# Loading all of x but its first 128 columns over ScalarE's DMA queue in a one-core encoder layer

## The chip, the core and the metric

The kernel runs on one core of one Trainium2 chip. The metric is the device time of one execution in microseconds (us), lower is better. Times come from runs without a profile. The rows come from one profiled execution of the kernel before.

## What is computed

One layer of a streaming encoder, on x of 512 rows by 1024 columns, all in float32. The part around the change is the first norm and the first projection:

```
hn   = rmsnorm(x, norm_mix_g)            # x * rsqrt(mean(x*x)) * g
proj = hn @ w_in                         # (512 x 1024) @ (1024 x 3592)
fq, fk, fv, ff, gq, gf, gi, gg = split(proj)
h = x + concat(fox_attention(fq, fk, fv, ff), hgrn2(gq, gf, gi) * silu(gg)) @ w_out
h = h + memory_cross_attention(rmsnorm(h), rmsnorm(mem))
h = h + square(relu(rmsnorm(h) @ w1)) @ w2
out = rmsnorm(h)
```

## The kernel before

Matrix products are made of two-part numbers. A weight panel of 1024 rows by 256 columns is loaded as two halves of 512 rows ("a" and "b", tiles `wr..`). ScalarE copies each into a rounded part (`wh..`, line 166), VectorE makes the remainder (`wl..`, line 168), and three matmuls (lines 227 to 229) stand for one product. The stretch of the change is the first 25 us.

x lies in one tile `xt`. For each of its eight blocks of 128 columns, `x_T(c)` (line 399) makes four TensorE transposes into a PSUM tile `xn`, `x_hi(c)` on ScalarE (line 402) and `x_lo(c)` on VectorE (line 405) turn that into the two parts `hn_hi` and `hn_lo`. The orders of TensorE, ScalarE and VectorE are written out by hand here: `x_T(0)`, `x_T(1)`, then the cast of the first weight quarter, then the parts of blocks 0 and 1. After that a loop over c makes the six matmuls of block c into the two accumulators `gf`, and then the transposes and parts of block c + 2, with other jobs behind them (`jobs`). Six matmuls `warm` stand ahead of all that on TensorE, and need no loaded data.

Loads are issued by an engine's own queue, in program order, SyncE's (SP) for nearly all. The first panel is loaded in four quarters of 256 KB (`load_next(4, ...)`), and the hook `more_x` puts a piece of x behind each of the first three. So SP's queue holds x[0:128] (256 KB), the first quarter of the weights, x[128:256] (256 KB), x[256:512] (512 KB), the second quarter, x[512:768] (512 KB), the third quarter, x[768:1024] (512 KB), the last quarter: 3 MB. Behind them come five small loads (`rows`) and the halves of the next panel (`wr1a`, `wr1b`). ScalarE's queue holds one small load (`gmr`), issued ahead of the engine's table load. Loads over SP and ScalarE take their completion semaphores in turn from a set of eight, DMAHW0 to DMAHW7; a load that gets one for the second time waits on its issuing engine until the load that had it before has landed.

Of the kernel before, what the change touches and what calls it, by code (L numbers as in the profile page):

```python
# [16 lines left out]
P = 128  # L17
# [5 lines left out]
WT = 256  # L23
# [19 lines left out]
def emit(  # L43
# [21 lines left out]
    nc = tc.nc  # L65
    te, ve, ac, gp = nc.tensor, nc.vector, nc.scalar, nc.gpsimd

    x, mem, w_in, w_out = x[0], mem[0], w_in[0], w_out[0]
# [36 lines left out]
    def t2(name, dt=F32, shape=(S,)):  # L105
        return t2p.tile([P] + list(shape), dt, tag="t2", name=name)
# [65 lines left out]
    def load_unit(name, spec, ks, parts=1, between=None):  # L172

        nw = max(sl.stop for sl, _ in spec)
        hi, lo = new_parts([UK, nw], name)
        raw_ = wrp.tile([P, UK * nw], F32, tag="wr", name=f"wr{name}", padded_shape=[P, UK * UW])
        raw_ = raw_.rearrange("p (k n) -> p k n", k=UK)
        nk = UK // parts
        splits = []
        for q in range(parts):  # L180
            qs, src_ks = slice(q * nk, (q + 1) * nk), slice(ks.start + q * nk, ks.start + (q + 1) * nk)
            for sl, src in spec:
                nc.sync.dma_start(raw_[:, qs, sl], src[:, src_ks, :])
            if between is not None:
                between(q)
            splits.append(split_of(hi[:, qs, :], lo[:, qs, :], raw_[:, qs, :]))
        return (hi, lo), splits

    def load_next(parts=2, between=None):

        i = len(stream)
        if i >= len(specs):
            return []
        units, splits = [], []
        for n in range(2):
            note = None if between is None else (lambda q, n=n: between(n * parts // 2 + q))
            unit, some = load_unit(f"{i}{'ab'[n]}", specs[i], slice(n * UK, (n + 1) * UK), parts // 2, note)
            units.append(unit)
            splits += some
        stream.append(tuple([u[x] for u in units] for x in range(2)))  # L200
        return splits
# [98 lines left out]
    xt = ap_.tile([P, NT, D], F32, tag="act", name="xt")  # L300
    gmr = t2("gmr", F32, (P,))[0:KC, :]
    ac.dma_start(gmr, norm_mix_g[0].rearrange("(k p) -> k p", p=P))

    def load_x(g, n=WT):
        gs = slice(g, g + n)
        nc.sync.dma_start(xt[:, :, gs], x[:, gs].rearrange("(t p) n -> p t n", p=P))

    def more_x(q):
        if q == 0:
            load_x(P, P)  # L310
        if q < 3:
            load_x((q + 1) * WT)

    load_x(0, P)
    first = load_next(4, more_x)
    rows = t2("rows", F32, (P,))[0:33, :]
    for r, src in ((0, norm_x_g), (8, norm_mem_g), (16, norm_ff_g)):
        nc.sync.dma_start(rows[r : r + 8, :], src[0].rearrange("(k p) -> k p", p=P))
# [590 lines left out]
    for n in range(len(units) + LAG):  # L909
        if n < len(units):  # L910
            p, tb, j = units[n]
# [492 lines left out]
```

## Time and profile before

| what | value |
|---|---|
| median of 3 runs | 786.74 us (785.2 to 787.53) |
| profiled execution, its own time | 784.74 us |
| span of its trace, first to last instruction | 783.0 us |
| TensorE busy | 770.4 us |
| HBM read | 88.14 MB |

The span leaves out some 1.7 us around the first and last instruction. A share of busy time is an average over all stages, so the first stage is to be read from its own rows. In a row of the timeline the first number is the start from the span's beginning, the second is a length, both in us; "xt<-in_x_dram" is the tile written and what is read; in square brackets stands how long the engine was idle before it and what it waited for. On a DMA queue's row (SPq, ACTq) the length is that of the issue, not of the transfer.

### The profile page before, as it was taken

To read this page: it belongs to the slowest core of one execution; us is meant where nothing else is said; L and a number is where in the kernel's file an instruction comes from. 1 tells how busy PE (TensorE), PEld (TensorE's weight loads), DVE (VectorE), ACT (ScalarE), POOL (GpSimd) and SP (SyncE) were. 2 spreads that over 40 slices of the span, in tenths; PEclk is the share of its full clock that TensorE was granted. 3 is DMA by queue.
4 is the path that set the end of the run, shared out by engine and by line. 5 is a ranking of instruction groups with operands and counts; after the bars stand their busy time and mean duration, and the time that the engine had idled before them with its cause. 6 is when DMAs were issued, how large, how long until landed. Compare 5 with 4: busy or idle time off the path is not lost.

```text
span 783.0 us, 11532 instructions
## 1 busy us (share of the span) xinstructions
PE 770.4 (98%) x4380; PEld 655.1 (84%) x4380; DVE 519.9 (66%) x839; ACT 367.6 (47%) x626; POOL 184.8 (24%) x259
## 2 busy tenths in 40 slices
PE   8999999999999999999999999999999999999996
PEld 5889998978989988888888888888888888888875
DVE  4746755687577656645538646959596877778662
ACT  5655455675565443244434344435353534344433
POOL 7106332414433005410006420100101010100013
PEclk9999999999999999999999999999999999999999
DMA  7543322242443443312222596575748475753302
GB/s 238 193 123 107 98 56 55 82 115 75 162 135 122 148 136 108 107 55 81 70 65 81 179 264 150 155 177 157 183 150 200 136 197 136 194 146 111 77 1 108
DMA packets 80777, 100.43 MB, mean 128 GB/s; under 512 B 4513, under 2 KB 62410, under 8 KB 80722
## 3 DMA queue, kind: packets, MB, share of 16 engines
q1 hardware_dynamic: 72002, 76.08, 30.7%
q0 software_dynamic: 8128, 22.57, 13.5%
q10 hardware_dynamic: 592, 1.05, 0.4%
q8 instruction: 34, 0.56, 0.3%
q14 instruction: 21, 0.17, 0.1%
HBM read 88.14 MB, written 4.21 MB: 118 GB/s over the span
## 4 chain that ended last, share of the span: by engine, by line
PE 96%; DVE 1%; DMA 1%; ACT 1%; issue 0%; POOL 0%; SPq 0%; POOLq 0%
PE u L229 7%; PE u L227 7%; PE u L228 7%; PE U L1280 3%; PE U L1279 3%; PE U L1278 3%; PE xq L227 2%; PE xw L227 2%; PE xw L229 2%; PE xq L229 2%; PE xq L228 2%; PE xw L228 2%; PE wo L227 2%; PE wo L228 2%; PE wo L229 2%; PE Y L1280 2%
## 5 line engine op out<-in xcount | busy, mean ns | idle before, releaser
L168 DVE TENSOR_TENSOR wld<-wq,whd 128x1024 fp32r<-128x1024 f32 x49 | 59.7, 1219 | 24.5 <-ACT whd L166 24.4
L227 PE MATMUL u<-x_hi,whu 128*128 128x512 f32 x192 | 74.7, 389 | 0.0
L228 PE MATMUL u<-x_lo,whu 128*128 128x512 f32 x192 | 74.7, 389 | 0.0
L229 PE MATMUL u<-x_hi,wlu 128*128 128x512 f32 x192 | 74.7, 389 | 0.0
L166 ACT ACTIVATE whd<-wq 128x1024 fp32r<-128x1024 f32 x49 | 51.0, 1051 | 23.7 <-PE u L228 22.1
L166 ACT ACTIVATE whu<-wru 128x1024 fp32r<-128x1024 f32 x24 | 25.3, 1052 | 56.8 <-DMA wru<-in_w_dram 56.8
L168 DVE TENSOR_TENSOR wlu<-wru,whu 128x1024 fp32r<-128x1024 f32 x24 | 29.3, 1220 | 26.4 <-ACT whu L166 26.2
L1156 POOL DMA_DIRECT2D wq<-wq x14 | 12.3, 878 | 136.7 <-DVE wld L168 96.9
L1156 POOL DMA_DIRECT2D wq<-in_w_dram x14 | 17.0, 1217 | 114.4 <-DMA wq<-in_w_dram 99.2
L1278 PE MATMUL U<-whd,hb 128*128 128x512 f32 x112 | 43.6, 389 | 0.0
L1279 PE MATMUL U<-wld,hb 128*128 128x512 f32 x112 | 43.6, 389 | 0.0
L1280 PE MATMUL U<-whd,hb 128*128 128x512 f32 x112 | 43.6, 389 | 0.0
L228 PEld LDWEIGHTS u<-x_lo,whu 128*128 128x128 f32 x192 | 36.0, 188 | 7.5
L227 PEld LDWEIGHTS u<-x_hi,whu 128*128 128x128 f32 x192 | 36.0, 188 | 7.5
L229 PEld LDWEIGHTS u<-x_hi,wlu 128*128 128x128 f32 x192 | 36.0, 188 | 7.4
L1216 ACT ACTIVATE sq<-ur 128x512 f32<-128x512 f32 x32 | 20.0, 626 | 29.1 <-DVE ur L1213 29.1
L1213 DVE SCALAR_TENSOR_TENSOR ur<-u,rbc 128x512 f32<-128x512 f32 x32 | 21.9, 688 | 17.2 <-PE u L229 17.2
L850 POOL TENSOR_SCALAR bi<-nF,Ft 128x128 f32<-128x128 f32 (+3 forms) x32 | 21.3, 664 | 43.0 <-PE pt L877 25.2
L867 ACT ACTIVATE bi<-bi,mx 128x128 f32<-128x128 f32 (+3 forms) x32 | 17.9, 560 | 20.9 <-DVE mx L865 20.6
L1279 PEld LDWEIGHTS U<-wld,hb 128*128 128x128 f32 x112 | 21.0, 188 | 4.4
L1278 PEld LDWEIGHTS U<-whd,hb 128*128 128x128 f32 x112 | 21.0, 188 | 4.4
L1280 PEld LDWEIGHTS U<-whd,hb 128*128 128x128 f32 x112 | 21.0, 188 | 4.3
(950 smaller groups left out, 2452.6 us busy)
## 6 DMA issues: line engine op xcount, KB each, us to landing
wq<-in_w_dram SPq DMA_DIRECT2D x39, 512.0 KB, 3.3
wru<-in_w_dram SPq DMA_DIRECT2D x24, 512.0 KB, 3.8
wq<-in_w_dram POOLq DMA_DIRECT2D x14, 512.0 KB, 8.7
wq<-wq POOLq DMA_DIRECT2D x14, 512.0 KB, 4.6
xTd<-xT POOLq DMA_DIRECT2D x4, 512.0 KB, 3.0
nF<-Fd POOLq DMA_DIRECT2D x8, 256.0 KB, 3.8
hT<-xTd POOLq DMA_DIRECT2D x4, 512.0 KB, 3.5
xt<-in_x_dram SPq DMA_DIRECT2D x3, 512.0 KB
```

What stands on the lines that cost most here:

```text
L166: ac.activation(hi, raw, AF.Copy)
L168: ve.tensor_tensor(lo, raw, f(hi), ALU.subtract)
L227: te.matmul(ps, wh, hi, start=n_ == 0, stop=False)
L228: te.matmul(ps, wh, lo, start=False, stop=False)
L229: te.matmul(ps, wl, hi, start=False, stop=n_ == KC - 1)
L850: gp.tensor_scalar(bi[:, 0:n], fF[h][:, 0:n], -1.0, Ft[:, tb, h : h + 1], op0=ALU.mult, op1=ALU.add)
L1156: gp.dma_start(raw.rearrange("p (k n) -> p k n", k=2), src, accum_op=ALU.add)
L1213: ve.scalar_tensor_tensor(u, ps, 0.0, rbc2, op0=ALU.max, op1=ALU.mult)
L1216: ac.activation(sqs[g, j][:, i, :], u, AF.Square)
L1278: te.matmul(ps, hi, whi[:, k, :], start=first_ and k == 0, stop=False, skip_group_check=True)
L1279: te.matmul(ps, hi, wlo[:, k, :], start=False, stop=False, skip_group_check=True)
L1280: te.matmul(ps, lo, whi[:, k, :], start=False, stop=k == 1, skip_group_check=True)
```

## The change

All pieces of x but the first are now issued over ScalarE's queue, ahead of the weights in the program. The hook `more_x` goes, so that the four weight quarters follow x[0:128] directly on SP.

```diff
-    def load_x(g, n=WT):
+    def load_x(g, n=WT, queue=ac):
         gs = slice(g, g + n)
-        nc.sync.dma_start(xt[:, :, gs], x[:, gs].rearrange("(t p) n -> p t n", p=P))
-
-    def more_x(q):
-        if q == 0:
-            load_x(P, P)
-        if q < 3:
-            load_x((q + 1) * WT)
-
-    load_x(0, P)
-    first = load_next(4, more_x)
+        queue.dma_start(xt[:, :, gs], x[:, gs].rearrange("(t p) n -> p t n", p=P))
+
+    load_x(0, P, nc.sync)
+    load_x(P, P)
+    for q in range(1, 4):
+        load_x(q * WT)
+    first = load_next(4)
```

ScalarE, from the start of the program, before (L166 is the cast of a weight quarter, L402 `x_hi`):

```order
L302 DMA gmr_113<-in_norm_mix_g_dram 8x128
L166 ACT_TABLE_LOAD
L166 ACTIVATE wh0a_116<-wr0a_118 128x512 [waits DMAHW2_49]
L402 ACTIVATE hn_hi_187<-xn0_205,g_mix_201 128x512 [waits DVE_49,PE_49]
L402 ACTIVATE hn_hi_187<-xn1_210,g_mix_201 128x512 [waits PE_49]
L402 ACTIVATE hn_hi_187<-xn2_229,g_mix_201 128x512 [waits PE_49]
L166 ACTIVATE wh0a_116<-wr0a_118 128x512 [waits DMAHW5_49]
```

The same place in the changed kernel, whose lines below the edit have numbers that are 3 lower (L399 is `x_hi`):

```order
L302 DMA gmr_113<-in_norm_mix_g_dram 8x128
L306 DMA xt_112<-in_x_dram 128x4x128
L306 DMA xt_112<-in_x_dram 128x4x256 x2
L306 DMA xt_112<-in_x_dram 128x4x256 [waits DMAHW2_49]
L166 ACT_TABLE_LOAD
L166 ACTIVATE wh0a_120<-wr0a_122 128x512 [waits DMAHW3_49]
L399 ACTIVATE hn_hi_187<-xn0_205,g_mix_201 128x512 [waits DVE_49,PE_49]
L399 ACTIVATE hn_hi_187<-xn1_210,g_mix_201 128x512 [waits PE_49]
L399 ACTIVATE hn_hi_187<-xn2_229,g_mix_201 128x512 [waits PE_49]
L166 ACTIVATE wh0a_120<-wr0a_122 128x512 [waits DMAHW5_49]
```

Four issues now stand ahead of the table load, and the fourth of them (x[768:1024]) has a wait. DMAHW2 is the semaphore of x[128:256] there.

SP's queue from the start, before (L183 loads weights, L306 x):

```order
L306 DMA xt_112<-in_x_dram 128x4x128
L183 DMA wr0a_118<-in_w_in_dram 128x2x256
L306 DMA xt_112<-in_x_dram 128x4x128
L306 DMA xt_112<-in_x_dram 128x4x256
L183 DMA wr0a_118<-in_w_in_dram 128x2x256
L306 DMA xt_112<-in_x_dram 128x4x256
L183 DMA wr0b_126<-in_w_in_dram 128x2x256
L306 DMA xt_112<-in_x_dram 128x4x256 [waits DMAHW0_49]
L183 DMA wr0b_126<-in_w_in_dram 128x2x256 [waits DMAHW1_49]
...
L319 DMA rows_130<-in_hgrn_norm_g_dram 1x128 [waits DMAHW5_49]
L320 DMA rows_130<-in_hgrn_lb_logits_dram 8x128 [waits DMAHW6_49]
L183 DMA wr1a_274<-in_w_in_dram 128x4x256 [waits DMAHW7_49,DVE_49]
```

And in the changed kernel:

```order
L306 DMA xt_112<-in_x_dram 128x4x128
L183 DMA wr0a_122<-in_w_in_dram 128x2x256 x2
L183 DMA wr0b_127<-in_w_in_dram 128x2x256
L183 DMA wr0b_127<-in_w_in_dram 128x2x256 [waits DMAHW0_49]
L315 DMA rows_130<-in_norm_x_g_dram 8x128 [waits DMAHW1_49]
...
L316 DMA rows_130<-in_hgrn_norm_g_dram 1x128 [waits DMAHW5_49]
L317 DMA rows_130<-in_hgrn_lb_logits_dram 8x128 [waits DMAHW6_49]
L183 DMA wr1a_274<-in_w_in_dram 128x4x256 [waits DMAHW7_49,DVE_49]
```

The four pieces of x are gone from between the weights. In the kernel before, DMAHW5 belonged to the second weight quarter and DMAHW6 to x[512:768], DMAHW7 to the third quarter; now DMAHW7 belongs to x[512:768].

One more thing moves by itself, on GpSimd (POOL), where the scheduler sets the order. Before, the small load `fb` (128 copies of 8 numbers) is issued near the start:

```order
masks.py:199 AFFINE_SELECT ident<-ident 128x128 [waits Pool_49]
L380 AFFINE_SELECT tri<-tri 128x128 [waits Pool_49]
L377 TENSOR_TENSOR id_182<-ident 128x64 [waits Pool_49]
L385 DMA fb<-in_fox_f_bias_dram 128x8
L367 MEMSET mkf_150 128x384
```

In the changed kernel the masks (`mkf`) come first, and `fb` stands after them:

```order
L369 AFFINE_SELECT mkf_166<-mkf_166 128x64
L374 TENSOR_TENSOR id_182<-ident 128x64
L377 AFFINE_SELECT tri<-tri 128x128
L370 AFFINE_SELECT mkf_166<-mkf_166 128x64 [waits Pool_49]
L382 DMA fb<-in_fox_f_bias_dram 128x8
```

So `fb` leaves the first microseconds. The orders of TensorE and VectorE are the same in both kernels, apart from the numbers of the semaphores.

## Rows read from the trace of the kernel before

**Rows 1.** Page, parts 1 and 4: busy shares, and the chain that ended last.

```profile
PE 770.4 (98%) x4380; PEld 655.1 (84%) x4380; DVE 519.9 (66%) x839; ACT 367.6 (47%) x626; POOL 184.8 (24%) x259
...
PE 96%; DVE 1%; DMA 1%; ACT 1%; issue 0%; POOL 0%; SPq 0%; POOLq 0%
```

**Rows 2.** The chain that ended last, first 30 us: start, length, what.

```profile
2.32 7.60 DMA xt<-in_x_dram
...
9.96 0.67 PE xn L399 x4
```

**Rows 3.** Timeline of SP's queue from the start: start, length of the issue, line, transfer.

```profile
0.79 0.42 SPq L306 DMA_DIRECT2D xt<-in_x_dram  x1
1.27 0.50 SPq L183 DMA_DIRECT2D wr0a<-in_w_in_dram  x1
1.81 1.01 SPq L306 DMA_DIRECT2D xt<-in_x_dram  x2
...
3.93 0.90 SPq L183 DMA_DIRECT2D wr0b<-in_w_in_dram  x1
...
5.82 2.03 SPq L183 DMA_DIRECT2D wr0b<-in_w_in_dram  x1
...
10.69 0.22 SPq L319 DMA_DIRECT2D rows<-in_hgrn_norm_g_dram  x1
12.21 0.27 SPq L320 DMA_DIRECT2D rows<-in_hgrn_lb_logits_dram  x1
13.02 0.40 SPq L183 DMA_DIRECT2D wr1a<-in_w_in_dram  x1
```

**Rows 4.** Timeline of ScalarE and its queue from the start.

```profile
0.79 0.61 ACTq L302 DMA_DIRECT2D gmr<-in_norm_mix_g_dram  x1
1.44 1.28 ACT L166 ACT_TABLE_LOAD   x1 [1.44 <-PEq L1390]
5.20 0.63 ACT L166 ACTIVATE wh0a<-wr0a 128x512 fp32r<-128x512 f32 x1 [2.48 <-DMA wr0a<-in_w_in_dram]
...
17.13 1.05 ACT L422 ACTIVATE x0j<-xt 128x1024 f32<-128x1024 f32 x1
```

**Rows 5.** Timeline of TensorE from the start.

```profile
1.30 2.74 PE L327 MATMUL warm<-zero 128*128 128x512 bf16 x6 [1.30 <-DVE zero L324]
...
4.32 1.11 PE L399 MATMUL xn<-ident,xt 128*128 128x128 f32 x4
6.03 0.66 PE L399 MATMUL xn<-ident,xt 128*128 128x128 f32 x4 [0.59 <-DMA xt<-in_x_dram]
6.46 0.49 PE L227 MATMUL gf<-hn_hi,wh0a 128*128 128x512 f32 x1
...
8.07 0.40 PE L228 MATMUL gf<-hn_lo,wh0a 128*128 128x512 f32 x1
8.30 0.39 PE L229 MATMUL gf<-hn_hi,wl0a 128*128 128x512 f32 x1
9.96 0.66 PE L399 MATMUL xn<-ident,xt 128*128 128x128 f32 x4 [1.27 <-DMA xt<-in_x_dram]
...
14.07 0.60 PE L399 MATMUL xn<-ident,xt 128*128 128x128 f32 x4
```

**Rows 6.** DMA issues: transfer, queue, count, KB each, median us from issue to landing.

```profile
out_dram<-fo SPq DMA_DIRECT2D x4, 256.0 KB, 2.6
xt<-in_x_dram SPq DMA_DIRECT2D x2, 256.0 KB, 2.8
wr0b<-in_w_in_dram SPq DMA_DIRECT2D x2, 256.0 KB, 9.1
```

**Rows 7.** Timeline, end of the span: both output queues, and TensorE's last matmul.

```profile
775.67 0.28 PE L1296 MATMUL y<-whd7b,hb 128*128 128x256 f32 x1
...
778.83 0.37 ACTq L1322 DMA_DIRECT2D out_dram<-fo  x1
778.86 0.33 SPq L1324 DMA_DIRECT2D out_dram<-fo  x1
```

**Rows 8.** Windows: stretch, length, busy of five engines, granted TensorE clock, DMA share, GB/s.

```profile
776.00:780.00 4.00, 0.00 (x0) 0.00 (x0) 1.16 (x2) 1.23 (x3) 0.85 (x2) 1.00 0.08 30
780.00:781.00 1.00, 0.00 (x0) 0.00 (x0) 0.00 (x0) 0.00 (x0) 0.00 (x0) 0.67 1.01 387
```

**Rows 9.** Timeline of ScalarE at a later table load, and the activation behind it.

```profile
155.34 1.28 ACT L867 ACT_TABLE_LOAD   x1
156.63 0.40 ACT L867 ACTIVATE bi<-bi,mx 128x128 f32<-128x128 f32 x1
```

## The prediction

> **What bounds the kernel now.** I read the busy shares first: TensorE is busy for 770.4 of 783.0 us, and 96% of the chain that ended last is its own [rows 1]. So a load matters only where TensorE stands still for it, and a standstill at the start moves all that follows by its length. The chain of the first 30 us shows one: 7.60 us of DMA into xt, up to 9.96 [rows 2]. Then the timeline of TensorE: it waits 0.59 us for x[128:256] (until 6.03) and 1.27 us for x[256:512] (until 9.96); from 14.07 on it goes from block to block with no wait shown [rows 5]. Last, the timelines of the two queues, for what stands in front of what [rows 3, 4].
>
> The landings in the order of SP's queue, read from whoever stopped waiting, with the sum of KB issued up to there: first weight quarter, 512 KB, 5.20 [rows 4]; x[128:256], 768 KB, 6.03 and x[256:512], 1280 KB, 9.96 [rows 5]; second quarter, 1536 KB, 10.69; x[512:768], 2048 KB, 12.21; third quarter, 2304 KB, 13.02, the wait of wr1a [rows 3]; last quarter, 3072 KB, 14.9, from its issue at 5.82 plus 9.1 [rows 3, 6]. I use this list as a scale: a transfer that ends when so many KB in all have been moved lands at about that time. It is an estimate, since it was made with one queue.
>
> **What must be in time.** The transposes of block 2 stand behind the six matmuls of block 0, and the first of these began 1.26 us after the first weight cast did (6.46 against 5.20), the last at 8.30 [rows 4, 5]. One step takes 0.23 us (8.07 to 8.30), so TensorE was free for block 2 at 8.53, or 3.33 us after that cast's start. The cast had until 9.96 - 3.33 = 6.63 to begin, and began at 5.20 [rows 4, 5]: 1.43 us to spare.
>
> **What the change adds on ScalarE.** Four issues stand ahead of its table load, and the fourth waits for x[128:256] to land, because its semaphore is given out a second time. Behind that wait stand the table load, the first cast, and the parts of blocks 0 and 1, for which VectorE and TensorE wait. The three issues without a wait end by about 2.9 us: 1.40 (0.79 + 0.61, [rows 4]) plus three at 0.5 (1.01 for two, [rows 3]); that is hidden, as nothing there is needed before 5.20. The wait is not hidden. With L for the landing of x[128:256], the cast begins at L + 0.05 + 0.47 (one issue; 0.42 to 0.50 where the queue is not full, 0.90 where it is, [rows 3]) + 0.04 + 1.28 (table load, [rows 4]) = L + 1.84.
>
> L is not in the trace. At the least it is 4.2: issue at 1.40 plus 2.8 for 256 KB with nothing in front [rows 4, 6]. At the most it comes after x[0:128] and all weights, at 1536 KB on the scale: 10.69. Between them I look at the only place where both queues carry like loads: the last two outputs, 256 KB each, are issued 0.03 us apart on ScalarE's and SP's queues [rows 7], the SP ones land 2.6 us after issue, against 2.8 for one alone [rows 6], and 387 GB/s flow meanwhile [rows 8]. So neither queue stands behind the other, and I take half of the flow for each. x[128:256] starts 0.6 us later than x[0:128], so by its end SP has moved 256 KB and a lead of some 150, 660 in all. If the queues take turns row by row, x's 512-byte rows against the weights' 1 KB rows, SP gets more, and it is some 830. The middle, about 750, is where this load stood before (768), so I leave L at 6.03.
>
> The rule of the Trainium skill, DMA: Bandwidth & Descriptors, section "Issuing engines are not separate DMA queues", speaks against the change: loads from several engines run on the same 16 DMA engines and interleave, and only the time to issue them is saved. The pair of outputs agrees. By that rule the forecast stands; were it wrong, the early landing below would be the likelier case.
>
> **The sum.** The cast begins at 6.03 + 1.84 = 7.87, TensorE is free for block 2 at 7.87 + 3.33 = 11.20, 1.24 us later than 9.96. x[256:512] itself: by half shares 512 KB of it come with 512 KB of weights, so it ends at 750 + 1024 = 1774 KB, on the scale 10.69 + 238/512 x (12.21 - 10.69) = 11.40 [rows 3]. The later of the two decides: 11.40, which is **1.44 us later**. Before, this load had only 1280 KB up to its end: it was near the front of one queue, and now shares with weights that are not needed yet.
>
> What is gained is worth nothing. The second quarter lands sooner, but its cast stands on ScalarE behind `x_hi(2)`, which follows block 2's transposes; the third and last quarters were waited for by no engine that mattered. What comes later is covered: x[512:768] ends at 1280 + 1280 = 2560 KB, some 13.7 on the scale, and is needed at 14.07 + 1.44 = 15.5 [rows 5]; wr1a's issue, which now waits for it, still waits for VectorE's work as well and moves no more than the rest; x[768:1024] ends last, at 14.9, and the sum of squares that reads it came at 17.13 [rows 4], now 18.6. If that cover were gone, each would cost its own lateness. The move of fb is off every wait in the first 60 us; I cost it at nothing, but it may quicken the loads.
>
> After block 2 every engine is shifted alike, so 1.44 us reach the end: 784.74 + 1.44 = 786.18 for an execution like the profiled one. That one lies 2.00 below the median of 786.74, within what single runs differ by; on the median it is **788.2 us**.
>
> **Rivals.**
>
> *The clock falls (slower).* TensorE would stand still from 6.69 (end of block 1's transposes, 6.03 + 0.66, [rows 5]) to 7.87 + 1.26 = 9.13: 2.44 us, where the longest standstill before was 1.27 and left it at full speed. For it: after the last matmul, over at 775.95 [rows 7], the granted clock holds 1.00 (2.4 GHz) over 776 to 780 and is 0.67 on the mean in the next microsecond [rows 8], so a standstill of about 4 us does bring 1.2 GHz. Against it: 2.44 lies nearer to 1.27 than to 4. Price: at the start the engine is slow from 1.30 until at least 5.43, by the same four transposes taking 1.11 us at 4.32 and 0.66 at 6.03 [rows 5]; 4.1 us at half speed lose 2.1 us of work. 786.74 + 1.44 + 2.1 = 790.3. It decides once that standstill counts as idle, and grows if x[128:256] is late.
>
> The Trainium skill, TensorE: Matmul & The Clock Gate, Part 1, says that the throttled state is the default and activity releases it; the trace's end agrees, and no row shows it for 2.44 us.
>
> *Early landing (no change).* If ScalarE's queue gets all it can take, x[128:256] lands at 4.2, the cast begins at 6.04 and TensorE is free at 9.37; x[256:512] then ends at 1024 KB, on the scale 8.0 [rows 5]. Gain 0.59: 786.2. The sequence on ScalarE allows no more, so a gain over 0.3% (2.36 us, about what a measurement of this kernel can tell from no change) is not in this change.
>
> *The weights go first (slower).* With L at 10.69 block 2 starts at 10.69 + 1.84 + 3.33 = 15.86: 5.90 later, 792.6. SP issues first and its queue holds 1280 KB, but the pair of outputs speaks against it.
>
> *A longer table load (slower).* In the trace the activation behind a table load starts 0.01 us after it ends [rows 9], so a wait behind the load would be a new one; if one as long as the load (1.28) came, the cast would begin at 9.15 and block 2 at 12.48: 2.52 later, 789.3. The Trainium skill, ScalarE: Activation LUTs, section "What ACT_TABLE_LOAD costs", adds a drain of about 1.38 us to each load, and by it block 2 would come at 12.58; the row at 155.34 shows none.
>
> **How the numbers follow.** Forecast 0.50 (of it 0.43 within 0.3%, 0.07 slower, since 788.2 is 0.9 below the bound of 789.1 and runs scatter by 1); clock 0.22 (0.20 slower, 0.02 within); early landing 0.17 (0.14 within, 0.03 faster by scatter); weights first 0.07, all slower; table load 0.04 (0.03 slower, 0.01 within). In sum: faster 0.03, same 0.60, slower 0.37. The range leaves out the weights-first case (0.07), the upper end of the clock case (0.05) and the lower half of the early landing (0.07): 785.9 to 790.6.
>
> **What would show it.** Right: ScalarE's table load stands behind the issue of x[768:1024] at about 6.1 to 6.6, the first cast starts near 7.9, block 2's transposes near 11.4, and from there every row is some 1.4 us later. Block 2's transposes waiting for DMA says that sharing decides; starting right after the matmuls says that the table load does. Wrong: a cast before 6.6 (no loss), gf matmuls 0.43 us apart instead of 0.23 (the clock), x[128:256] after 7 (the weights).

## The result, and the profile after

| | before | after |
|---|---|---|
| median, us (10 runs each) | 785.28 (783.8 to 787.53) | 787.45 (786.47 to 788.69) |
| ratio, 95% interval | | 1.0032 (1.0023 to 1.0041) |
| profiled execution, us | 784.74 | 786.47 |
| its span, us | 783.0 | 784.8 |

The change makes the kernel slower by 2.5 us (1.8 to 3.2, from the ratio). The prediction was 1.44 us more, at 788.2, and it gave "within 0.3%" 0.60 and "slower" 0.37. The measured time lies in its range. The ratio is just past the bound of 0.3%, with an interval that reaches to both sides of it, so between those two cases it decides nothing. But the loss is larger than the sum of 1.44, by an amount that the rest of this document looks for.

The page after, parts 1 and 4, beside [rows 1]: TensorE is busy 1.3 us more, and the chain is its own as before.

```profile
PE 771.7 (98%) x4380; PEld 656.2 (84%) x4380; DVE 519.6 (66%) x839; ACT 367.5 (47%) x626; POOL 184.0 (23%) x259
PE 96%; ACT 1%; DVE 1%; DMA 1%; issue 0%; POOL 0%; ACTq 0%; POOLq 0%
```

The timeline of ScalarE and its queue after, beside [rows 4] (start, length, then in brackets the idle time ahead of it and its releaser):

```profile
1.43 4.78 ACTq L306 DMA_DIRECT2D xt<-in_x_dram  x4
6.24 1.28 ACT L166 ACT_TABLE_LOAD   x1 [6.24 <-DMA xt<-in_x_dram]
7.54 0.63 ACT L166 ACTIVATE wh0a<-wr0a 128x512 fp32r<-128x512 f32 x1
```

The four issues of x take 4.78 us since the fourth waits; the table load, which stood at 1.44, stands at 6.24, and the first cast at 7.54 instead of 5.20. The timeline of TensorE after, beside [rows 5]:

```profile
5.86 0.66 PE L396 MATMUL xn<-ident,xt 128*128 128x128 f32 x4 [0.46 <-DMA xt<-in_x_dram]
8.80 0.80 PE L227 MATMUL gf<-hn_hi,wh0a 128*128 128x512 f32 x1 [2.28 <-ACT hn_hi L399]
...
11.06 0.63 PE L228 MATMUL gf<-hn_lo,wh0a 128*128 128x512 f32 x1
11.48 0.63 PE L229 MATMUL gf<-hn_hi,wl0a 128*128 128x512 f32 x1
11.91 0.69 PE L396 MATMUL xn<-ident,xt 128*128 128x128 f32 x4
```

Three things are to be seen. TensorE stands still from 6.52 (5.86 + 0.66) to 8.80, released by ScalarE's `hn_hi`. The matmuls behind it start 0.42 us apart (11.06 to 11.48) where they stood 0.23 apart [rows 5]. And block 2's transposes at 11.91 have no bracket: no load is waited for. They come 1.95 us later than at 9.96. The windows after, by microsecond (length, busy of PE, PEld, DVE, ACT, POOL, granted clock, DMA share, GB/s) give the reason for the wide spacing:

```profile
8.00:9.00 1.00, 0.20 (x1) 0.20 (x1) 0.80 (x2) 1.00 (x3) 1.00 (x2) 0.83 1.11 349
9.00:10.00 1.00, 0.98 (x2) 0.48 (x3) 1.00 (x2) 0.32 (x1) 1.00 (x4) 0.50 1.10 349
...
11.00:12.00 1.00, 1.00 (x4) 0.64 (x3) 0.00 (x0) 0.00 (x0) 1.00 (x6) 0.50 0.84 261
12.00:13.00 1.00, 1.00 (x8) 0.91 (x7) 0.00 (x0) 0.36 (x1) 0.98 (x3) 0.96 0.00 1
```

The granted clock is 0.83 on the mean of the microsecond from 8, in which TensorE stands still until 8.80; it is 0.50 (1.2 GHz) from 9 to 12, and back at 2.4 GHz in the 13th microsecond. So the 1.95 us have two parts. From the cast's start until TensorE was free for block 2 took 3.33 us before; at that pace block 2 would start at 7.54 + 3.33 = 10.87, 0.91 late. It took 4.37, and the other **1.04 us** are the clock's. Of the 1.95 us, 1.8 are left at the end of the span.

### The profile page after: what moved, and what is told of

Read it like the earlier page. It is cut to its first block, busy times and chain, and to the rows that moved or that the text cites. A ratio compares the mean times of both kernels' runs of the same rounds, so it can differ in the third digit from the quotient of the medians.

```text
span 784.8 us, 11535 instructions
## 1 busy us (share of the span) xinstructions
PE 771.7 (98%) x4380; PEld 656.2 (84%) x4380; DVE 519.6 (66%) x839; ACT 367.5 (47%) x626; POOL 184.0 (23%) x259
## 4 chain that ended last, share of the span: by engine, by line
PE 96%; ACT 1%; DVE 1%; DMA 1%; issue 0%; POOL 0%; ACTq 0%; POOLq 0%
PE u L227 7%; PE u L229 7%; PE u L228 7%; PE U L1277 3%; PE U L1275 3%; PE U L1276 3%; PE xq L227 2%; PE xw L227 2%; PE xw L229 2%; PE xq L228 2%; PE xq L229 2%; PE xw L228 2%; PE wo L227 2%; PE wo L228 2%; PE wo L229 2%; PE Y L1277 2%
## 5 line engine op out<-in xcount | busy, mean ns | idle before, releaser
L166 ACT ACTIVATE whd<-wq 128x1024 fp32r<-128x1024 f32 x49 | 51.1, 1052 | 23.4 <-PE u L228 23.4
L166 ACT ACTIVATE whu<-wru 128x1024 fp32r<-128x1024 f32 x24 | 25.3, 1053 | 57.6 <-DMA wru<-in_w_dram 57.6
```

The source lines that it names most:

```text
L166: ac.activation(hi, raw, AF.Copy)
```

## The experiments

| run | what differs | median, us | ratio to before (95%) |
|---|---|---|---|
| `a2_again` | the changed kernel once more | 787.94 | 1.0033 (1.0022 to 1.0043) |
| `e2_last_on_sp` | change without the wait | 784.39 | 0.9992 (0.9983 to 1.0000) |
| `e1_longer_wait` | change with another, longer wait | 789.09 | 1.0049 (1.0037 to 1.0061) |
| `e3_fill_idle` | change, TensorE kept busy | 786.39 | 1.0018 (1.0007 to 1.0030) |
| `e5_fb_early` | change, `fb` early again | 788.55 | 1.0038 (1.0023 to 1.0052) |
| `e6_split_fb_early` | no wait, `fb` early | 785.63 | 1.0007 (0.9996 to 1.0018) |
| `e4_fb_late` | before, `fb` late | 784.43 | 0.9989 (0.9980 to 0.9998) |
| `e7_fb_late_fill` | before, `fb` late, three fillers | 783.63 | 0.9977 (0.9968 to 0.9986) |
| `b7_again` | `e7_fb_late_fill` once more | 783.40 | 0.9973 (0.9963 to 0.9984) |
| `e8_split_fill` | no wait, three fillers | 783.80 | 0.9984 (0.9976 to 0.9993) |

The kernel before had a median of 784.87 to 785.17 beside these. All kernels do the whole computation; the fillers are added matmuls of zeros into a PSUM tile that the first real product overwrites.

**Is it the wait on ScalarE?** `e2_last_on_sp` puts the last piece of x behind the weights on SP, so that ScalarE issues three loads and none of them waits.

```diff
-    for q in range(1, 4):
+    for q in range(1, 3):
         load_x(q * WT)
     first = load_next(4)
+    load_x(3 * WT, WT, nc.sync)
```

> The changed kernel with x[768:1024] issued on SyncE's queue behind the weights: ScalarE issues three pieces of x and waits for none. Theory (the wait ahead of the table load, and the clock that falls in the standstill): table load at about 2.9 us, first cast at about 5.2 when the weights land, block 2's transposes at 9.3 to 9.5 when x[256:512] lands, clock at 2.4 GHz throughout; 2.3 to 3.0 us faster than the changed kernel, 0.4 to 0.8 faster than before. Rival (the shared queues): block 2 still waits for x[256:512] at 11 us or later, and the time stays within 0.5 us of the changed kernel.

It ran at the time of the kernel before, or a little under it. ScalarE's timeline in that run:

```profile
1.43 1.53 ACTq L306 DMA_DIRECT2D xt<-in_x_dram  x3
2.99 1.28 ACT L166 ACT_TABLE_LOAD   x1 [2.99 <-issue]
5.22 0.63 ACT L166 ACTIVATE wh0a<-wr0a 128x512 fp32r<-128x512 f32 x1 [0.95 <-DMA wr0a<-in_w_in_dram]
```

The table load is at 2.99, and the first cast waits for its weights as it did before. The whole loss is gone with the fourth issue, and a little more: 1.0032 against 0.9992, 0.0040 or 3.1 us. Three issues of x on ScalarE's queue do not cost it. Block 2's transposes came at 9.64, behind slow matmuls and without a wait for a load, where 9.3 to 9.5 and such a wait had been expected.

`e1_longer_wait` also takes the fourth issue away from the table load, and puts it behind the first cast, where its semaphore is that of the third weight quarter, which lands later.

```diff
-    for q in range(1, 4):
+    for q in range(1, 3):
         load_x(q * WT)
...
         first[0]()
+        load_x(3 * WT)
         x_hi(0)
```

> The changed kernel, with the issue of x[768:1024] put behind the first weight cast on ScalarE. Its semaphore is then the one of the third weight quarter, so ScalarE waits there for that quarter (about 9 us in the changed kernel) and not for x[128:256] (5.8 us); the table load and the first cast stand ahead of the wait. Theory (what stands behind the wait on ScalarE sets the time): the table load comes at about 2.8 us, but the parts of block 0 only at about 9.5, the matmuls of gf at about 10.2, block 2's transposes at 13 to 13.3 with the clock at 1.2 GHz for some of it; 1.0 to 1.5 us slower than the changed kernel, 3 to 3.5 slower than before. Rival (the shared queues set the time, by the landing of x[256:512]): the landings stay as in the changed kernel, and so does the time.

Measured 3.9 us slower by the ratio (2.9 to 4.8), a little more than expected. The timeline of that run, rows of ScalarE, its queue and TensorE:

```profile
5.00 0.63 ACT L166 ACTIVATE wh0a<-wr0a 128x512 fp32r<-128x512 f32 x1 [0.72 <-DMA wr0a<-in_w_in_dram]
...
8.93 0.38 ACTq L306 DMA_DIRECT2D xt<-in_x_dram  x1
9.41 1.27 ACT L399 ACTIVATE hn_hi<-xn,g_mix 128x512 fp32r<-128x512 f32 x2 [3.78 <-DMA wr0b<-in_w_in_dram]
10.15 0.79 PE L227 MATMUL gf<-hn_hi,wh0a 128*128 128x512 f32 x1 [3.73 <-ACT hn_hi L399]
```

The table load and the cast are early here, and yet everything behind the waiting issue is late: ScalarE stands 3.78 us for a landing that none of its own work needs. The cost goes with the landing that the issue waits for, not with the queue that carries x; part of it is the clock, which reads 0.50 to 0.51 from 8 to 14 in that run.

**How much of it is the clock?** `a2_again` and `e3_fill_idle` ask that. The first is the changed kernel unaltered.

> The changed kernel as it is, once more, for a second profiled execution and beside the next runs. Theory (ScalarE's wait for x[128:256], and the clock that falls in the standstill of some executions): 2.0 to 2.7 us slower than before; the first cast 1.7 us behind the landing of x[128:256], wherever that lies between 5.8 and 7.3 us; gf's first matmuls 0.43 us apart where the clock is down, 0.23 where it is not.

The span of its profiled execution is 787.2, 2.4 more than that of the first profile. The timeline of it, rows of ScalarE and TensorE:

```profile
6.78 1.28 ACT L166 ACT_TABLE_LOAD   x1 [6.78 <-DMA xt<-in_x_dram]
8.07 0.63 ACT L166 ACTIVATE wh0a<-wr0a 128x512 fp32r<-128x512 f32 x1
...
9.33 0.80 PE L227 MATMUL gf<-hn_hi,wh0a 128*128 128x512 f32 x1 [2.28 <-ACT hn_hi L399]
...
12.44 1.06 PE L396 MATMUL xn<-ident,xt 128*128 128x128 f32 x4
...
15.73 0.49 PE L396 MATMUL xn<-ident,xt 128*128 128x128 f32 x3
```

and the window over its slow stretch (the last three numbers are granted clock, DMA share and GB/s):

```profile
9.00:15.00 6.00, 5.66 (x15) 4.17 (x16) 2.49 (x5) 2.06 (x4) 4.82 (x14) 0.50 0.54 160
```

x[128:256] landed half a microsecond later than in the first profile, and the same 2.28 us of waiting brought 1.2 GHz from 9 to 15 instead of 9 to 12. Block 2's transposes are 4.37 us behind the cast again (clock 1.04), and from block 2 to block 3 it takes 3.29 (12.44 to 15.73) where the first profile has 1.91 (11.91 to 13.82): 1.38 more. So the clock cost 1.04 us in one execution and 2.4 in the other, and the wait itself 0.91 and 8.07 + 3.33 - 9.96 = 1.44. Sums of 1.95 and 3.9 against spans that are 1.8 and 4.2 us above the 783.0 of before; the median loss of 2.5 lies between.

`e3_fill_idle` puts ten bf16 matmuls of zeros ahead of the first product, in the time in which TensorE would stand still.

```diff
         gfps = [mm(f"gf{i}") for i in range(2)]
+        for _ in range(10):
+            te.matmul(gfps[0], zero[:, 0:P], zero, start=True, stop=True)
         gfg = [gemm_fm(gfps[i], wt0, i * P, hn_hi, hn_lo) for i in range(2)]
```

> The changed kernel with ten more matmuls of 512 columns on TensorE ahead of the first matmul of gf, into an accumulator that is started anew behind them. They need no loaded data, and fill the standstill of 6.5 to 8.8 us. Theory (the clock falls in that standstill and costs about 1.0 us): granted clock 1.00 throughout, gf's matmuls 0.23 us apart from the first on, block 2's transposes at about 10.9 in place of 11.9; 0.5 to 1.0 us faster than the changed kernel, since not every execution of it may have fallen. Rival (the clock comes down anyway, or its cost is hidden by a landing): block 2 at 11.9, time as the changed kernel.

TensorE's timeline:

```profile
7.31 1.12 PE L396 MATMUL xn<-ident,xt 128*128 128x128 f32 x4 [1.88 <-DMA xt<-in_x_dram]
8.22 3.25 PE L439 MATMUL gf<-zero 128*128 128x512 bf16 x10
11.12 0.58 PE L227 MATMUL gf<-hn_hi,wh0a 128*128 128x512 f32 x1
11.54 0.39 PE L228 MATMUL gf<-hn_lo,wh0a 128*128 128x512 f32 x1
11.77 0.39 PE L229 MATMUL gf<-hn_hi,wl0a 128*128 128x512 f32 x1
```

and the window in which the clock was down in the first profile:

```profile
9.00:10.00 1.00, 1.00 (x4) 0.37 (x3) 0.35 (x1) 1.00 (x2) 1.00 (x4) 1.00 1.09 346
```

With TensorE busy the clock stays at 1.00 and the products are 0.23 us apart (11.54 to 11.77). The median falls from 787.45 to 786.39, 0.0014 or 1.1 us by the ratios. That is what is left of the clock's price after the fillers' own: the cast began at 8.99, so the first product could have come at 8.99 + 1.26 = 10.25, and the fillers held it until 11.12, by 0.87. So the clock costs some 1.1 to 2.0 us on the median, and the wait the rest of the 3.1. The intervals of the two ratios overlap, and the 0.87 is from one execution, so the split is rough; that the clock has a part in the loss is read from the spacing, not from the medians. x[128:256] landed only at 7.3 in this execution, so that block 2 came at 12.70 and not at 10.9, and the wait's price moves with that from one execution to the next: 0.91 and 1.44 above, and by the same reckoning 8.99 + 3.33 - 9.96 = 2.36 here.

**Did the move of `fb` matter?** The prediction costed it at nothing. `fb` is 4 KB, 128 copies of 32 bytes, over GpSimd's queue, and the change moved it from 2.08 us to 11.96. `e4_fb_late` does only that to the kernel before: a copy from a mask that is made late holds the load back, to 14.22 us.

```diff
     fb = cp.tile([P, FH], F32, name="fb")
+    gp.tensor_copy(fb, mku[:, 1, 0, 0:FH])
     gp.dma_start(fb, fox_f_bias[0].partition_broadcast(P))
```

> The kernel before, with only the small load fb (128 copies of 8 numbers, on GpSimd's queue) made to come behind the masks, at about 14 us, by a copy into its tile ahead of it. All of x stays on SyncE. Question: what slowed the loads of the kernel before to about 235 GB/s between 3 and 8 us, where the changed kernel has 345 from 4 us on. Theory fb: 340 GB/s from 3 or 4 us on, x[256:512] lands at about 8.3 to 8.7 in place of 9.9, block 2 follows its matmuls at 8.6 to 8.8, and the kernel is 1.0 to 1.4 us faster than before. Theory queues (one queue alone is slow at the start): rates and time as before, x[256:512] at 9.9.

`e5_fb_early` is the changed kernel with `fb` first on GpSimd, and `e6_split_fb_early` is `e2_last_on_sp` with the same line:

```diff
-    gp.dma_start(fb, fox_f_bias[0].partition_broadcast(P))
+    with ahead(400):
+        gp.dma_start(fb, fox_f_bias[0].partition_broadcast(P))
```

> The changed kernel with one thing undone: the small load fb is issued first of all on GpSimd, as in the kernel before it was near the start (2.1 us), and not behind the masks (12 us). Theory (fb slows the loads it meets, whichever queue they are in): 180 to 260 GB/s between 4 and 8 us in place of 350, x[256:512] lands at 11 us or later in place of 9.3, block 2's transposes at 12 to 12.5, and the kernel is 0.3 to 1 us slower than the changed one. Rival (two queues make the loads quicker by themselves): rates, landings and time as in the changed kernel.

> Three pieces of x on ScalarE's queue, x[768:1024] on SyncE's behind the weights (so no wait on ScalarE), and fb first on GpSimd: the sharing of the queues alone, without the wait and without the move of fb. Theory fb, with sharing as the prediction had it: x[256:512] lands at about 11 to 11.6, later than in the kernel before (9.9), block 2 waits for it, and the kernel is 0.8 to 1.5 us slower than before. Rival (sharing costs nothing, it was fb that made the difference of the two kernels in loads and the queues are served alike): block 2 at 9.5 to 10, same time as before.

The windows over 4 to 8 us, in which all the large loads are under way, give these rates in GB/s, each from one profiled execution:

| x over | `fb` early | `fb` late |
|---|---|---|
| SP alone | before 224 | `e4_fb_late` 322, `b7_again` 296, `e7_fb_late_fill` 288 |
| SP and ScalarE | `e5_fb_early` 254, `e6_split_fb_early` 255 | after 353, `a2_again` 347, `e2_last_on_sp` 351, `e1_longer_wait` 349, `e3_fill_idle` 348, `e8_split_fill` 348 |

The rows of two pairs that differ in `fb` alone: before,

```profile
4.00:8.00 4.00, 2.99 (x14) 2.14 (x14) 2.08 (x4) 1.90 (x3) 4.00 (x12) 1.00 0.84 224
```

and `e4_fb_late`;

```profile
4.00:8.00 4.00, 3.00 (x12) 2.29 (x12) 1.61 (x3) 1.72 (x3) 4.00 (x12) 1.00 0.99 322
```

`e2_last_on_sp`,

```profile
4.00:8.00 4.00, 3.39 (x13) 2.50 (x13) 1.76 (x4) 2.16 (x4) 4.00 (x12) 1.00 1.09 351
```

and `e6_split_fb_early`.

```profile
4.00:8.00 4.00, 2.51 (x13) 1.96 (x13) 1.52 (x3) 1.97 (x4) 4.00 (x13) 1.00 1.04 255
```

With `fb` early the loads flow at 224 to 255 GB/s, with `fb` late at 288 to 353, on one queue or two: the move of `fb` is the larger part of the difference. The number of queues has a part as well, since among the late ones those with two queues have 347 to 353 and those with one 288 to 322. In its worst microsecond in `e5_fb_early` 73 GB/s are left, at a DMA share of 0.65 (window of that run):

```profile
5.00:6.00 1.00, 0.00 (x0) 0.00 (x0) 0.00 (x0) 0.00 (x0) 1.00 (x3) 1.00 0.65 73
```

x[128:256], for which TensorE waits until 5.86 and 6.39 in the two profiles of the changed kernel, comes at 7.38 in that run; but it comes at 7.31 in `e3_fill_idle` with `fb` late, so this one landing does not tell what `fb` does.

The landing of x[256:512] says more. It is read from the small load on SP's queue that takes its semaphore, and with x on SP alone and `fb` late that row gives only a bound, since SP was not waiting any more. The landings in us:

| x over | `fb` early | `fb` late |
|---|---|---|
| SP alone | before 9.96 | by 7.84 (`e4_fb_late`), 8.08 (`b7_again`), 8.38 (`e7_fb_late_fill`) |
| SP and ScalarE | 10.34 (`e6_split_fb_early`), 10.39 (`e5_fb_early`) | 8.85 (`e8_split_fill`), 9.20 (`e1_longer_wait`), 9.31 (after), 9.49 (`e2_last_on_sp`), 9.56 (`a2_again`), 10.35 (`e3_fill_idle`) |

The bound in the timeline of SP's queue in `e4_fb_late`:

```profile
7.84 0.29 SPq L318 DMA_DIRECT2D rows<-in_norm_ff_g_dram  x1
```

So with x on SP alone the move of `fb` brings this load at least 1.6 to 2.1 us sooner; with two queues it is some 0.9 on the middle value (9.4), and nothing in `e3_fill_idle`. And with `fb` late in both, the second queue makes the load later: by 1.3 us or more between the middle values (9.4 and 8.08). Single executions with two queues lie 1.5 us apart, so these are rough.

The Trainium skill, DMA: Bandwidth & Descriptors, section "Specifications", puts the least size for line rate at 512 bytes, with a read-modify-write below it. `fb`'s 32-byte pieces are far under that, and the trace agrees as far as it goes: before, `fb`'s 4 KB took 6.7 us to land, where 256 KB of x took 2.8 [rows 6]. That such a load slows those on other queues is what these rows add. Whether it is the size of its pieces that does it, or that it comes over GpSimd's queue, no run here tells apart.

In time `fb` is small: `e6_split_fb_early` against `e2_last_on_sp`, 1.0007 against 0.9992, is 1.2 us, `e5_fb_early` against `a2_again` 0.6 by the medians, within the intervals (and in `e5_fb_early` the clock was down from 7.4 on, after TensorE's wait for x[128:256]), and `e4_fb_late` saves 0.9 us (0.2 to 1.6). Block 2's transposes in the timeline of `e6_split_fb_early`,

```profile
10.36 0.66 PE L398 MATMUL xn<-ident,xt 128*128 128x128 f32 x4 [1.50 <-DMA xt<-in_x_dram]
```

and of `e4_fb_late`:

```profile
9.76 0.60 PE L400 MATMUL xn<-ident,xt 128*128 128x128 f32 x4
```

Sharing with `fb` early brings x[256:512] at 10.36 instead of 9.96: 0.4 us, and the time 0.5 us (-0.3 to 1.4) above before. That 0.4 is too low a price for sharing, since `fb` is issued at 1.32 there and lands in 5.7 us, at 7.0, where it landed at 2.08 + 6.7 = 8.8 before and slowed the loads for longer. Both landings with `fb` early are sooner than was expected (11 or later). In `e4_fb_late` the bracket is gone: block 2 waits for no load, and its start is set by block 0's matmuls, which are slow there (next).

**A version better than both.** In `e4_fb_late` and `e2_last_on_sp` the first products start 0.43 us apart until 9.5 and 9.6, because TensorE's slow start lasts longer than in the profile of before. `e7_fb_late_fill` adds three fillers between the first two groups of transposes to `e4_fb_late`, and `b7_again` is the same kernel beside `e8_split_fill`, which adds them to `e2_last_on_sp`.

```diff
+        gfps = [mm(f"gf{i}") for i in range(2)]
         x_T(0)
+        for _ in range(3):
+            te.matmul(gfps[0], zero[:, 0:P], zero, start=True, stop=True)
         x_T(1)
...
-        gfps = [mm(f"gf{i}") for i in range(2)]
```

> The kernel before with fb behind the masks, and three more matmuls of 512 columns between the transposes of blocks 0 and 1, where TensorE waits for x[128:256]. In the run with fb late alone the matmuls of block 0 were still 0.43 us apart until 9.2 us. Theory (TensorE is slow at first until it has been busy for long enough, and a standstill puts that off): gf's matmuls 0.23 us apart from about 7 us on in more executions, block 2 at 8.8 to 9.2, 0.2 to 0.8 us faster than fb late alone, 0.7 to 1.3 faster than before. Rival: the extra matmuls only push block 1 and block 0 back: same as fb late alone or up to 0.6 slower.

> The kernel before with fb late and three filler matmuls, once more, so that it stands beside the run of the next label on one chip. Expected 783.6 as in its first run, 1.0 to 1.5 us under the kernel before; block 2's transposes at 9.0 to 9.1, right behind block 0's matmuls, which are 0.23 us apart from the second on.

> The changed kernel with x[768:1024] on SyncE's queue behind the weights (so nothing waits ahead of ScalarE's table load) and the same three filler matmuls between the first two groups of transposes. fb stays where the changed kernel has it, behind the other loads. It tells what the division of the loads over two queues is worth once its wait and the slow start of TensorE are taken away. If the division costs nothing and gains nothing: 783.6, as the kernel of the label before, with block 2's transposes at 9.0 to 9.5. If sharing the flow with the weights delays x[256:512]: its landing is after 9.5, a wait for DMA of 0.2 to 0.7 us stands ahead of block 2's transposes, and the time is 0.2 to 0.7 us above that of the label before.

TensorE's rows for block 0's last product and block 2's transposes, in `b7_again`

```profile
8.12 0.39 PE L229 MATMUL gf<-hn_hi,wl0a 128*128 128x512 f32 x1
8.35 0.60 PE L400 MATMUL xn<-ident,xt 128*128 128x128 f32 x4
```

and in `e8_split_fill`:

```profile
8.17 0.40 PE L229 MATMUL gf<-hn_hi,wl0a 128*128 128x512 f32 x1
8.88 0.66 PE L397 MATMUL xn<-ident,xt 128*128 128x128 f32 x4 [0.32 <-DMA xt<-in_x_dram]
```

`e7_fb_late_fill` and `b7_again` beat both kernels, by 1.8 and 2.1 us on the kernel before. With x on one queue and `fb` out of the way, block 2 starts right behind the products, at 8.35 here and at 9.06 in the profile of `e7_fb_late_fill`. With two queues it waits 0.32 us for x[256:512] (until 8.88, earlier than expected), and the median is 0.4 us higher, both as sharing was expected to cost; the intervals overlap, so the row shows this cost, in one execution, and the time does not.

## Why the prediction was right or wrong

*ScalarE's wait: right, and within 0.33 us.* It named the table load behind the fourth issue, with x[128:256] at 6.03, the cast at 7.87 and the first product at 9.13. Measured: a chain from 5.81 (1.43 + 4.38) over the issue, 0.38, to the cast at 7.54 and the product at 8.80. That L would stay near 6.03 was the choice between 4.2 and 10.69, and holds on the profile (5.81; 6.35 in `a2_again`). That it came so near is in part luck: it was read off the scale of KB that fails below, and in `e3_fill_idle`, with the same loads, it was 7.3. The chain of the changed kernel shows it link by link ("issue" is the stretch with the table load):

```profile
1.43 4.38 DMA xt<-in_x_dram
5.84 0.38 ACTq L306
6.34 1.20 issue
7.54 0.63 ACT wh0a L166
```

*x[256:512] at 11.40, the later of the two: wrong.* This is the step that failed, with the move of `fb` put at nothing in it, and 1.44 was taken from it. It landed by 9.31, where the third small load on SP's queue, which takes its semaphore, stops waiting: the timeline of that queue after,

```profile
9.31 0.27 SPq L315 DMA_DIRECT2D rows<-in_norm_ff_g_dram  x1
```

and TensorE's waits over the first 20 us (total, times, longest), where the only one for a load is that for x[128:256]:

```profile
PE gf L227 <- ACT hn_hi L399: 2.3, 1, 2.3
...
PE xn L396 <- DMA xt<-in_x_dram: 0.5, 1, 0.5
```

The first fault is the larger. The scale of KB was made while `fb` slowed the loads, and the change moved `fb` away; the prediction saw the move, said that it might quicken the loads, and left it out of the sum, where it is worth 1.6 us or more to this load. The second is that the scale took the queue's order for the amount that had flowed. The windows from the start to that landing, before,

```profile
0.00:9.96 9.96, 6.38 (x21) 3.09 (x21) 2.63 (x7) 3.18 (x4) 9.32 (x28) 1.00 0.76 216
```

after,

```profile
0.00:9.31 9.31, 5.18 (x16) 2.34 (x16) 1.64 (x6) 3.05 (x4) 8.68 (x27) 0.97 0.83 249
```

and in `e4_fb_late`, to the bound above:

```profile
0.00:7.84 7.84, 5.54 (x17) 2.87 (x18) 1.97 (x6) 2.84 (x4) 7.20 (x25) 1.00 0.74 223
```

216 GB/s over 9.96 us are 2.15 MB, where the scale has 1280 KB, 1.31 MB: pieces behind x[256:512] in the same queue were moving along with it. The Trainium skill, DMA: Bandwidth & Descriptors, section "Queues, rings and completion order", says that completion is not first in, first out for one issuing engine; these rows show loads that overlap, and none that overtakes another. After, 249 over 9.31 are 2.32 MB; in `e4_fb_late`, with `fb` late and one queue, 223 over 7.84 are 1.75 MB at the most. So with `fb` late sharing let 0.57 MB or more go by ahead of this load, some 1.6 us at 350 GB/s (an estimate from these windows). Sharing therefore does make this load later, as the prediction said, by 0.4 us or more with `fb` early and about 1.3 with `fb` late; the move of `fb` took that back, and block 2, held up by ScalarE's wait and the clock until 11.91, did not wait for the load.

*The clock: a rival at 0.22, and what came.* It was held less likely since 2.44 us of standing still was nearer to 1.27, which left the clock up, than to 4. In both profiles 2.28 us brought it down, and the sign that the prediction had named for it, products 0.43 us apart, is what came. Beside them, 2.45 us brought it down in `e5_fb_early` (0.69 from 7 to 8, then 0.50), and 1.50 in `e6_split_fb_early` and 1.88 in `e3_fill_idle` left it at 1.00. Its price was set at 2.1 from the slow start; it was 1.04 and 2.4. The rival's own time, 790.3, was 2.9 too high, and half of that, 1.46, is the median that it stood on (see the sum).

*The other rivals.* The landing at 4.2 and the weights first did not come (5.81). No second wait stands behind the table load: its 1.28 us from 6.24 end at 7.52, and the cast starts at 7.54. The covers for what lands later held, as far as TensorE's waits show: none of them names x[512:768] or x[768:1024].

*The sum.* What decided was ScalarE's wait, 1.24 in the prediction, and not the landing. 1.44 was right in sign and, against 0.91 and 1.44 for the wait alone in the two profiles, about right in size, but by a wrong step; the 1 to 2 us of the clock that bring it to 2.5 were left to a rival. And 788.2 stood on the median of the 3 runs shown, 786.74, which more runs put at 785.28: 1.46 us lower. The two misses have opposite signs, and so the time came out within 0.8 us of the forecast while the difference came out 1.1 us off: that the time is so near is luck.

## What to carry to other kernels

Count the loads that an engine's queue issues ahead of its own work against the completion semaphores that are there: the first that takes one for the second time makes the engine stand until an older load has landed, and here that was worth 3.1 us with the clock that fell meanwhile, all of it avoided by giving one load to another queue. When a wait moves a standstill on TensorE into the time before a dense stretch, price the clock with it, as the likely case where the standstill is longer than any that the trace shows to be harmless. And a scale taken from a trace holds only for what ran in it: here a 4 KB load that the change pushed aside moved the awaited transfer by as much as the sharing that the change is about.

## What the runs showed that I had not expected

- A 4 KB load in 32-byte pieces takes about a quarter of the flow from 3 MB of other loads over 4 us (254 and 255 against 347 to 353 GB/s with two queues, 224 against 288 to 322 with one).
- TensorE's slow start isn't in the column of the granted clock. In `e2_last_on_sp` the products are 0.43 us apart until 9.6 (9.22 and one step), as at 1.2 GHz in the profile after, while the window reads 1.00. The end of the slow start differs between executions: before 6.03 in the profile of before, by the transposes that take 0.66 us [rows 5], and 9.6 here. With three fillers between the transposes the products are 0.23 us apart (`b7_again`). Timeline of TensorE in `e2_last_on_sp`,

```profile
8.79 0.63 PE L228 MATMUL gf<-hn_lo,wh0a 128*128 128x512 f32 x1
9.22 0.63 PE L229 MATMUL gf<-hn_hi,wl0a 128*128 128x512 f32 x1
```

and its window:

```profile
8.00:9.60 1.60, 1.60 (x5) 1.02 (x4) 0.56 (x1) 0.00 (x0) 1.60 (x4) 1.00 1.10 348
```
